# A hybrid decoder layer: the 64x64 triangular inversions as 64x64 tiles of TensorE instead of block-diagonal 128x128 operands, and another place for one group's input strips

## The chip, the cores and the metric

One Trainium2 chip, of which the kernel uses one core. The metric is the device time of one execution in microseconds (us), and lower is better. The engines are named as in the profile: PE is TensorE's matmuls and PEld its weight loads, DVE is VectorE, ACT is ScalarE, POOL is GpSimd, SP issues nearly all DMAs.

## The reference

One layer of a recurrent decoder, for a prompt of 1024 tokens and 8 sample sequences of 8 tokens. The columns of `z = x @ w_in` go to four mixers A (RG-LRU), B (Mamba-2 SSD), C (gated DeltaNet) and D (S5); their outputs are gated, joined, multiplied by `w_out`, and normalised. The change concerns C's chunked form and the order of C's and D's first steps:

```python
def gdn_mixer(...):                       # C: 4 heads of width 64, chunks of 64 tokens
    qkv, new_buf = causal_conv(qkv, ...)  # width 4, 768 channels (6 strips of 128)
    ...
    kk = jnp.einsum('bzhtd,bzhsd->bzhts', k, k)
    m = jnp.where(strict, beta[..., :, None] * kk * gamma, 0.0)
    eye = jnp.eye(c, dtype=F32)
    tmat = lax.linalg.triangular_solve(eye + m, jnp.broadcast_to(eye, m.shape),
                                       left_side=True, lower=True, unit_diagonal=True)
    value = tmat @ (beta[..., None] * v)
    kcum = tmat @ ((beta * jnp.exp(decay))[..., None] * k)
    ...                                   # then a scan over chunks with the state s

def s5_mixer(...):                        # D: 16 groups, scan, then a gate by a 256x256 product
    ...
    y = jax.nn.gelu(y.reshape(bsz, L, W_D), approximate=False)
    y = y * jax.nn.sigmoid(jnp.einsum('ble,ef->blf', y, p['s5_glu_w']) + p['s5_glu_b'])
```

## The kernel before

Tokens are laid out as 64 sample tokens and 1024 prompt tokens. `gemm_block` makes one block of `x @ w_in`: 128 output channels (a strip) by 320 or 384 tokens, 24 matmuls, three for each of eight slices of the contraction (lines 232 to 234: high by high, low by high, high by low part). A strip has three blocks, so 72 matmuls.

**The order of the work.** The program is written as Python generators. `merge` takes the next step of the generator that has used the least, by the costs that the `yield`s give, over its weight. A scheduler then orders each engine's instructions at build time, by that order and its own estimates, and each engine works its list through in order. So the order on PE is fixed, and a matmul whose operand is late holds up all matmuls behind it.

**The first third.** `u_tiles` makes D's input strips. `s5` goes on in stages that end at a `yield`: half 0's scan, half 0's outputs and half 1's scan, half 1's outputs (line 683, stored by the `ydd` transfer and read back as `yt`), and the gate (GLU, lines 707 to 730; `gh` and `gl` are the high and low parts of its operands). Beside them C's six channel strips (`strip_c`) are made in the order 2, 3, 0, 1, 4, 5, and `in_c` makes those that are still missing, and for each its convolution (`conv_of`); `norms` (line 762) takes sums of squares with matmuls of two columns.

**The long middle.** `gdn` (C) and `side` (everything else: A, B, the gates, then the projection `project`) are merged with weights 130 and 280. C works on a sample tile of 64 rows (`ti` 0) and eight prompt tiles of 128 rows (`ti` 1 to 8). Each prompt tile holds two chunks of 64 tokens: rows 0 to 63 (`lo`) and 64 to 127 (`hi`), for four heads. For a tile, `prep` makes the matrix A, `invert` inverts its 64x64 diagonal blocks, `state` and `finish` use them.

**The inversion** doubles the size of the inverted blocks in six levels (three in the sample tile). `X` and `Y` are an approximate inverse and its transpose, f16, packed as 64 columns for each head. At each level PE makes `T` from `ah` (f16 of A) and X (line 863), DVE masks it with `lev` (line 865), PE adds products to X and Y in the bank `XY` (lines 870 and 873), and ACT copies X and Y out (lines 875 and 880). The two chunks of a tile are done by one 128x128 matmul for each head, so the stationary operand has to be block-diagonal, zero outside the blocks. `ah`, `al`, `tb` and `yb` are kept for that, cleared once; `spread` (line 854, DVE, two copies) puts T into `tb`, and two ACT copies (line 878) put Y into `yb`, except at the last level. One refinement follows: `E` (lines 884, 885), `F` (line 892); then two steps that join the chunks of a tile (line 896, already 64x64, and 906, 909).

Of the kernel before, what the change touches and what calls it, by code (L numbers as in the profile page):

```python
# [10 lines left out]
F16 = mybir.dt.float16  # L11
BF = mybir.dt.bfloat16
I32 = mybir.dt.int32
AF = mybir.ActivationFunctionType
OP = mybir.AluOpType
AX = mybir.AxisListType.X
PS = bass.MemoryType.PSUM
DR = bass.MemoryType.DRAM

P = 128  # L20
NP = 1024
NS = 64
T = NP + NS
# [29 lines left out]
def hybrid_step(ctx, tc, I, O, dbg=None):  # L53
    nc = tc.nc
    mm = nc.tensor.matmul
    tr = nc.tensor.transpose
    act = nc.scalar.activation
    V = nc.vector
    G = nc.gpsimd
    tt, ts, stt = V.tensor_tensor, V.tensor_scalar, V.scalar_tensor_tensor  # L60
# [16 lines left out]
    def nm(s):  # L77
        uid[0] += 1
        return f"{s}_{uid[0]}"

    def const(shape, dt=F32, name="c"):
        n = nm(name)
        return con.tile(shape, dt, name=n, tag=n)
# [18 lines left out]
    def bank(name="p", tag="b"):  # L102
        if tag == "e":
            tag = "bisibi"[turn[0] % 6]
            turn[0] += 1
        return pm.tile([P, 512], F32, name=nm(name), tag=tag, bufs=banks[tag])

    def run(g):
        for _ in g:
            pass  # L110
# [658 lines left out]
    def gdn(wk, up, q, k, v, rk, rq):  # L769
        def r1(name, tag="r", bufs=3):  # L770
            return wk.tile([P, 256], F32, name=nm(name), tag=tag, bufs=bufs)

        def f16(name, tag, n, bufs):
            return wk.tile([P, n], F16, name=nm(name), tag=tag, bufs=bufs)
# [10 lines left out]
        ts(rq2, rq2, 1.0 / 4096, None, op0=OP.mult)  # L785
        rq8 = const([P, 9, 4], F32, "rq8")
        ts(rq8, rq, 0.125, None, op0=OP.mult)
        ah, al, tb, yb = (wk.tile([P, 4, P], F16, name=t, tag=t) for t in ("ah", "al", "tb", "yb"))
        for t in (ah, al, tb, yb):
            G.memset(t, 0.0)  # L790
        S = const([P, 2, P], F32, "S")
        V.memset(S, 0.0)

# [42 lines left out]
        def invert(d):  # L836


            n, A = d["n"], d["A"]
            nb = n // 64  # L840
            lo, hi = slice(0, 64), slice(64, P)
            blocks = (lo, hi)[:nb]
            V.tensor_copy(ah[:n, :, lo], A[:n, :, lo])
            if nb == 2:
                V.tensor_copy(ah[hi, :, hi], A[hi, :, hi])
            for s in blocks:
                tt(al[s, :, s], A[s, :, s], ah[s, :, s], OP.subtract)

            def pk(z):
                return z.rearrange("p (h t) -> p h t", h=4)  # L850

            def spread(dst, src):
                for s in blocks:
                    V.tensor_copy(dst[s, :, s], src[s])

            idq = idp[:n].unsqueeze(1)
            px = bank("XY", "i")
            pX, pY = pk(px[:, :256]), pk(px[:, 256:])
            X = Y = None
            for l in range(3 if n == NS else 6):  # L860
                pt = pk(bank("T", "i")[:, :256])
                for h in range(4):
                    mm(pt[:n, h], ah[:n, h, :n], idp[:n] if X is None else X[:n, h], start=True, stop=True)  # L863
                t_ = pk(f16("T", "T", 256, 2))
                tt(t_[:n], pt[:n], lev[:n, l].unsqueeze(1).to_broadcast([n, 4, 64]), OP.mult)  # L865
                spread(tb, t_)
                if l == 0:
                    mm(px[:n].rearrange("p (a t) -> p a t", t=64), idh[:n, :n], idq.to_broadcast([n, 8, 64]), start=True, stop=False, skip_group_check=True)
                for h in range(4):
                    last = mm(pY[:n, h], tb[:n, h, :n], idp[:n] if Y is None else Y[:n, h], start=False, stop=h == 3, skip_group_check=True)  # L870
                with tc.issue_after(last.ins):
                    for h in range(4):
                        mm(pX[:n, h], idh[:n, :n] if Y is None else yb[:n, h, :n], t_[:n, h], start=False, stop=False, skip_group_check=True)  # L873
                X = pk(f16("X", "X", 256, 2))
                act(X[:n], pX[:n], AF.Copy)  # L875
                if l < (2 if n == NS else 5):
                    for s in blocks:
                        act(yb[s, :, s], pY[s], AF.Copy)  # L878
                Y = pk(f16("Y", "Y", 256, 2))
                act(Y[:n], pY[:n], AF.Copy)  # L880
                yield 0.2
            pe = pk(bank("E", "i")[:, :256])
            for h in range(4):
                mm(pe[:n, h], ah[:n, h, :n], X[:n, h], start=True, stop=False)
                mm(pe[:n, h], al[:n, h, :n], X[:n, h], start=False, stop=True)
            for s in blocks:
                tt(tb[s, :, s], pe[s], idp[s].unsqueeze(1).to_broadcast([64, 4, 64]), OP.subtract)
            yield 0.5
            pf = bank("F", "i")
            pF, pX1 = pk(pf[:, :256]), pk(pf[:, 256:])  # L890
            for h in range(4):
                mm(pF[:n, h], tb[:n, h, :n], Y[:n, h], start=True, stop=True)
            Yf = wk.tile([P, 4, P], F32, name=nm("Yf"), tag="py", bufs=3)
            if nb == 2:
                for h in range(4):
                    mm(pX1[lo, h], Y[lo, h], tb[lo, h, lo], start=True, stop=True)
            for s in blocks:
                tt(Yf[s, :, s], Y[s], pF[s], OP.subtract)
            yield 0.3
            if nb == 2:  # L900
                x1 = pk(r1("x1", "kh", 1))
                tt(x1[lo], X[lo], pX1[lo], OP.subtract)
                pj = bank("J", "i")
                pT_, pY_ = pk(pj[:, :256]), pk(pj[:, 256:])
                for h in range(4):
                    mm(pT_[hi, h], A[lo, h, hi], x1[lo, h], start=True, stop=True)
                act(x1[hi], pT_[hi], AF.Copy, scale=-1.0)
                for h in range(4):
                    mm(pY_[lo, h], x1[hi, h], Yf[hi, h, hi], start=True, stop=True)
                act(Yf[lo, :, hi], pY_[lo], AF.Copy)  # L910
                G.memset(Yf[hi, :, lo], 0.0)
                yield 0.9
            d["Y"] = Yf
# [323 lines left out]
    u_run, s5_run = u_tiles(), s5(dp)  # L1237
# [8 lines left out]
    idh = const([P, P], F16, "idh")  # L1246
# [3 lines left out]
    idp = const([P, 64], F16, "idp")  # L1250
# [17 lines left out]
    for l in range(6):  # L1268
        m = 1 << l
        nb = 64 // (2 * m)  # L1270
# [16 lines left out]
    z, early_z = {}, (2, 3, 0, 1, 4, 5)  # L1287

    def strip_c(i):
        z[i] = yield from gemm_strip(C_QKV, "cache_gdn_conv", i, cs)  # L1290

    next(s5_run)
    columns()
    for i in early_z[:1]:
        run(strip_c(i))
    next(s5_run)
    for i in early_z[1:3]:
        run(strip_c(i))
    next(s5_run)
    run(s5_run)  # L1300
    dec_c = decays(raw[:, :, 8:12], hv[:, 4:8], nega[:, 4:8])
    dec_b = decays(raw[:, :, 0:4], hv[:, 0:4], nega[:, 0:4])
# [31 lines left out]
    wk = ctx.enter_context(tc.tile_pool(name="wk", bufs=1, reuse_waits="tile"))  # L1334
# [215 lines left out]
```

## Time and profile before

| what | before |
|---|---|
| device time, median of 3 runs (lowest to highest) | 604.24 us (603.3 to 605.51) |
| the profiled execution: device time, span of its instructions | 608.82 us, 607.1 us |
| PE busy | 582.5 us (96%), 4284 matmuls |
| PEld busy | 505.9 us (83%) |
| DVE busy | 461.9 us (76%) |
| ACT busy | 320.7 us (53%) |
| mean granted TensorE clock | 0.979 |

All figures but the first row are of one profiled execution. Busy PE includes the time in which a matmul's result is still on its way through the array, so several matmuls are counted at once: how far PE is from its pace is seen in the distances between the starts of matmuls. A matmul with f32 operands that aren't rounded to the "fp32r" form stands twice in the trace.

### The profile page before, as it was taken

How to read it: one execution, taken by the hardware profiler on the slowest of the kernel's cores; microseconds unless marked ns; L12 is line 12 of the kernel's file. 1: busy time of each engine (PE TensorE's matmuls, PEld its weight loads, DVE VectorE, ACT ScalarE, POOL GpSimd, SP SyncE). 2: the span in 40 equal slices, each digit the busy share in tenths (PEclk: the TensorE clock that was granted, in tenths of full speed). 3: DMA queues.
4: the chain of work that ended last, by engine and by line, in shares of the span. 5: the costliest groups of instructions: out<-in, count | busy, mean ns of one | idle time of the engine just before them, and what ended most of it. 6: DMA issues, size and time to landing. Idle time of an engine off the chain costs nothing.

```text
span 607.1 us, 11704 instructions
## 1 busy us (share of the span) xinstructions
PE 582.5 (96%) x4284; PEld 505.9 (83%) x4284; DVE 461.9 (76%) x1372; ACT 320.7 (53%) x877; POOL 57.1 (9%) x165
## 2 busy tenths in 40 slices
PE   5999899998999999999999999999999999999995
PEld 4999899998999886888988888788887876888883
DVE  6997969964548676688887986878796879766655
ACT  5555245345335365979575575767666566222210
POOL 8120000000100010120010010010101001000000
PEclk9999899999789999999999999999999979999998
DMA  8552122041401110001032310100104132221221
GB/s 300 181 157 80 55 64 87 19 125 60 141 18 44 33 37 36 18 19 36 2 101 68 112 32 18 36 28 3 52 1 153 36 124 90 86 105 70 108 101 70
DMA packets 24186, 44.14 MB, mean 73 GB/s; under 512 B 3200, under 2 KB 10432, under 8 KB 24128
## 3 DMA queue, kind: packets, MB, share of 16 engines
q1 hardware_dynamic: 24128, 43.38, 21.8%
q8 instruction: 34, 0.56, 0.4%
q14 instruction: 24, 0.20, 0.1%
HBM read 32.97 MB, written 10.41 MB: 71 GB/s over the span
## 4 chain that ended last, share of the span: by engine, by line
PE 72%; DVE 15%; ACT 5%; issue 3%; DMA 3%; POOL 1%; SPq 1%; DVEq 0%; ACTq 0%; POOLq 0%
PE pg L233 8%; PE pg L232 8%; PE pg L234 8%; PE pg L1443 6%; PE pg L1442 6%; PE pg L1444 6%; PE kq L825 2%; PE ssq L762 1%; DMA wr<-in_w_tiles_dram 1%; DVE acc L268 1%; PE cb L1107 1%; PE pg L405 1%; DVE cm L471 1%; PE pg L406 1%; PE pg L407 1%
## 5 line engine op out<-in xcount | busy, mean ns | idle before, releaser
L232 PE MATMUL pg<-xh,wh 128*128 128x384 f32 (+1 forms) x432 | 149.4, 346 | 0.0
L233 PE MATMUL pg<-xl,wh 128*128 128x384 f32 (+1 forms) x432 | 148.2, 343 | 0.0
L234 PE MATMUL pg<-xh,wl 128*128 128x384 f32 (+1 forms) x432 | 148.0, 343 | 0.0
L232 PEld LDWEIGHTS pg<-xh,wh 128*128 128x128 f32 x432 | 83.1, 192 | 2.7 <-issue 1.3
L234 PEld LDWEIGHTS pg<-xh,wl 128*128 128x128 f32 x432 | 82.8, 192 | 1.7 <-issue 0.8
L233 PEld LDWEIGHTS pg<-xl,wh 128*128 128x128 f32 x432 | 83.0, 192 | 1.1 <-issue 0.3
L1443 PE MATMUL pg<-wol,wh 128*128 128x512 f32 (+1 forms) x144 | 57.6, 402 | 0.0
L1442 PE MATMUL pg<-woh,wh 128*128 128x512 f32 (+1 forms) x144 | 57.6, 401 | 0.0
L1444 PE MATMUL pg<-woh,wl 128*128 128x512 f32 (+1 forms) x144 | 57.6, 401 | 0.0
L268 DVE SCALAR_TENSOR_TENSOR acc<-z,pcol,acc 128x1112 f32<-128x1112 f32 x36 | 49.3, 1372 | 3.3 <-ACT acc L266 3.0
L156 ACT ACTIVATE wh<-wr 128x512 fp32r<-128x512 f32 (+1 forms) x40 | 25.3, 634 | 39.1 <-PE pg L233 32.6
L875 ACT ACTIVATE X<-XY 128x256 f16<-128x256 f32 (+1 forms) x51 | 19.6, 385 | 27.4 <-PE XY L873 27.3
L1444 PEld LDWEIGHTS pg<-woh,wl 128*128 128x128 f32 (+1 forms) x144 | 26.6, 184 | 7.4 <-issue 0.4
L1442 PEld LDWEIGHTS pg<-woh,wh 128*128 128x128 f32 (+1 forms) x144 | 26.5, 184 | 7.4 <-ACT woh L1407 0.4
L1443 PEld LDWEIGHTS pg<-wol,wh 128*128 128x128 f32 (+1 forms) x144 | 26.5, 184 | 7.3 <-issue 0.6
L246 ACT ACTIVATE z<-pg 128x384 f32<-128x384 f32 (+2 forms) x48 | 17.4, 394 | 25.7 <-PE pg L234 24.0
L878 ACT ACTIVATE yb<-XY 64x256 f16<-64x256 f32 x82 | 30.5, 372 | 0.8
L865 DVE TENSOR_TENSOR T<-T,lev 128x256 f16<-128x256 f32 (+1 forms) x51 | 21.5, 421 | 11.4 <-PE T L863 10.2
L157 DVE TENSOR_TENSOR wl<-wr,wh 128x512 fp32r<-128x512 f32 (+1 forms) x40 | 27.8, 694 | 2.0 <-ACT wh L156 1.8
L1445 DVE SCALAR_TENSOR_TENSOR y<-y,pg 128x512 f32<-128x512 f32 (+1 forms) x18 | 12.3, 683 | 15.8 <-PE pg L1444 15.8
L405 PE MATMUL pg<-wh,xh 128*128 128x268 f32 x72 | 21.4, 298 | 2.7 <-ACT bg L410 2.7
L1458 ACT ACTIVATE y<-y,nb,rs 128x1024 f32<-128x1024 f32 (+1 forms) x8 | 10.0, 1244 | 23.9 <-DVE nb L1457 12.8
(444 smaller groups left out, 1334.1 us busy)
## 6 DMA issues: line engine op xcount, KB each, us to landing
wr<-in_w_tiles_dram SPq DMA_DIRECT2D x40, 256.0 KB, 2.8
x<-in_x_t_dram SPq DMA_DIRECT2D x8, 544.0 KB, 4.8
wo<-in_w_out_dram SPq DMA_DIRECT2D x16, 256.0 KB, 3.0
y<-in_x_dram SPq DMA_DIRECT2D x8, 512.0 KB, 3.2
out_y_dram<-y SPq DMA_DIRECT2D x7, 512.0 KB, 2.6
bgd<-bg SPq DMA_DIRECT2D x9, 128.0 KB, 1.7
dud<-us SPq DMA_DIRECT2D x2, 544.0 KB, 4.6
U<-dud SPq DMA_DIRECT2D x16, 68.0 KB, 2.6
```

Source lines behind the costliest of these rows:

```text
L156: act(hv_, wv, AF.Copy)
L157: lo_eng[0].tensor_tensor(lv, wv, hv_.bitcast(F32), OP.subtract)
L232: mm(o, whi[k], xh[:, k, a:b], start=(k == 0), stop=False)
L233: mm(o, whi[k], xl[:, k, a:b], start=False, stop=False)
L234: mm(o, wlo[k], xh[:, k, a:b], start=False, stop=(k == 7))
L268: stt(acc[:, :CL], s[:, j:j + CL], col(wkey, j * nt + i), acc[:, :CL], OP.mult, OP.add)
L405: mm(o, xh[:, k, c0:c0 + P], whi[k], start=(k == 0), stop=False)
L865: tt(t_[:n], pt[:n], lev[:n, l].unsqueeze(1).to_broadcast([n, 4, 64]), OP.mult)
L878: act(yb[s, :, s], pY[s], AF.Copy)
L1442: mm(ps[:n], mh[k_], woh[:, k_, e], start=(k_ == 0), stop=False)
L1443: mm(ps[:n], mh[k_], wol[:, k_, e], start=False, stop=False)
L1444: mm(ps[:n], ml[k_], woh[:, k_, e], start=False, stop=(k_ == 7))
```

## The change

The inversion's products no longer run on the whole array. Each head's product is made as two 64x64 products, `lo` in the array's first rows and columns and `hi` in its last, one behind the other (`each`). So every group of four matmuls is now one of eight, and `tb`, `yb`, `spread`, the two ACT copies into `yb` and the clearing of the four tiles are gone. X's products now stand ahead of Y's. A level's cost for `merge` is 0.4 where it was 0.2. Apart from that, C's strips are made beside S5's stages as 1, 2, 0 and 2: five strips ahead of `in_c` where there were three.

```diff
-        ah, al, tb, yb = (wk.tile([P, 4, P], F16, name=t, tag=t) for t in ("ah", "al", "tb", "yb"))
-        for t in (ah, al, tb, yb):
-            G.memset(t, 0.0)
...
-            V.tensor_copy(ah[:n, :, lo], A[:n, :, lo])
-            if nb == 2:
-                V.tensor_copy(ah[hi, :, hi], A[hi, :, hi])
-            for s in blocks:
-                tt(al[s, :, s], A[s, :, s], ah[s, :, s], OP.subtract)
...
-            def spread(dst, src):
-                for s in blocks:
-                    V.tensor_copy(dst[s, :, s], src[s])
-
-            idq = idp[:n].unsqueeze(1)
+            def each(o, lhs, rhs, **kw):
+                for h in range(4):
+                    for s in blocks:
+                        last = mm(o[s, h], lhs(s, h), rhs(s, h), **kw)
+                return last
+
+            def of(z):
+                return lambda s, h: z[s, h]
+
+            ah, al = (pk(f16(t, t, 256, 1)) for t in ("ah", "al"))
+            for s in blocks:
+                V.tensor_copy(ah[s], A[s, :, s])
+            for s in blocks:
+                tt(al[s], A[s, :, s], ah[s], OP.subtract)
+            idq = lambda s, h: idp[s]
...
-                for h in range(4):
-                    mm(pt[:n, h], ah[:n, h, :n], idp[:n] if X is None else X[:n, h], start=True, stop=True)
+                each(pt, of(ah), idq if X is None else of(X), start=True, stop=True)
                 t_ = pk(f16("T", "T", 256, 2))
                 tt(t_[:n], pt[:n], lev[:n, l].unsqueeze(1).to_broadcast([n, 4, 64]), OP.mult)
-                spread(tb, t_)
...
-                for h in range(4):
-                    last = mm(pY[:n, h], tb[:n, h, :n], idp[:n] if Y is None else Y[:n, h], start=False, stop=h == 3, skip_group_check=True)
+                last = each(pX, idq if Y is None else of(Y), of(t_), start=False, stop=False, skip_group_check=True)
                 with tc.issue_after(last.ins):
-                    for h in range(4):
-                        mm(pX[:n, h], idh[:n, :n] if Y is None else yb[:n, h, :n], t_[:n, h], start=False, stop=False, skip_group_check=True)
-                X = pk(f16("X", "X", 256, 2))
+                    each(pY, of(t_), idq if Y is None else of(Y), start=False, stop=False, skip_group_check=True)
+                X, Y = (pk(f16(t, t, 256, 2)) for t in "XY")
                 act(X[:n], pX[:n], AF.Copy)
-                if l < (2 if n == NS else 5):
-                    for s in blocks:
-                        act(yb[s, :, s], pY[s], AF.Copy)
-                Y = pk(f16("Y", "Y", 256, 2))
                 act(Y[:n], pY[:n], AF.Copy)
-                yield 0.2
+                yield 0.4
...
-    for i in early_z[:1]:
+    for n in (1, 2, 0):
+        for i in early_z[len(z):len(z) + n]:
+            run(strip_c(i))
+        next(s5_run, None)
+    for i in early_z[len(z):len(z) + 2]:
         run(strip_c(i))
-    next(s5_run)
-    for i in early_z[1:3]:
-        run(strip_c(i))
-    next(s5_run)
     run(s5_run)
```

Three places of the order on the engines show what moves. The first is PE's list inside the inversion of the second prompt tile, level 1: `T` is the product's bank, `pg` a block of a strip of `side`; the last figure is the output's rows by columns. Before:

```order
L234 MATMUL pg_3495<-xh,wl_3291 128x384
L863 LDWEIGHTS ah
L863 MATMUL T_3366<-X_3346,ah 128x64
L863 LDWEIGHTS ah
L863 MATMUL T_3366<-X_3346,ah 128x64
L863 LDWEIGHTS ah
L863 MATMUL T_3366<-X_3346,ah 128x64
L863 LDWEIGHTS ah
L863 MATMUL T_3366<-X_3346,ah 128x64
L232 MATMUL pg_3495<-xh,wh_3290 128x384
```

And now (the group has eight pairs of a load and a matmul, behind a strip matmul; its last three pairs are shown, with what follows):

```order
L847 LDWEIGHTS ah_3401
L847 MATMUL T_3454<-X_3437,ah_3401 64x64
L847 LDWEIGHTS ah_3401
L847 MATMUL T_3454<-X_3437,ah_3401 64x64
L847 LDWEIGHTS ah_3401
L847 MATMUL T_3454<-X_3437,ah_3401 64x64
L233 MATMUL pg_3441<-xl,wh_3330 128x384
L234 MATMUL pg_3441<-xh,wl_3331 128x384
```

Four matmuls of the whole array have become eight of a quarter of it, and strip matmuls of the whole array still stand on both sides. Counted along the whole of PE's list, neighbours that use array tiles of different sizes number 178 before and 366 after, 188 more.

The second place is DVE's list at the same levels; `acc` is a convolution step over 1112 columns. Before:

```order
L865 TENSOR_TENSOR T_3371<-T_3366,lev_873 128x256
L1006 TENSOR_TENSOR oss_3712<-oss_3712,rq_407_2318 128x4
L268 SCALAR_TENSOR_TENSOR acc_4125<-z_3012,pcol_96,acc_4125 128x1112
L854 COPY tb<-T_3371 64x4x64 x2
L951 SCALAR_TENSOR_TENSOR R_3576<-ks_3571,nea_2316,vt_3178 128x64 x4
```

And now:

```order
L866 TENSOR_TENSOR T_3417<-T_3408,lev_873 128x256
L1213 SCALAR_TENSOR_TENSOR gi_3254<-gi_3254,acc_2802 128x1112
L268 SCALAR_TENSOR_TENSOR acc_4246<-z_2931,pcol_96,acc_4246 128x1112
L866 TENSOR_TENSOR T_3463<-T_3454,lev_873 128x256
L268 SCALAR_TENSOR_TENSOR acc_4246<-z_2931,pcol_96,acc_4246 128x1112
```

Between a level's mask and its next products there was a second visit to DVE, here behind a convolution step; now there is one visit.

The third place is PE's list ahead of D's gate (`glu`). Before:

```order
L233 MATMUL pg_2138<-xl,wh_2107 128x384
L234 MATMUL pg_2138<-xh,wl_2108 128x384
L725 MATMUL glu_1721<-gh_1712,gh_1708 128x320
L725 MATMUL glu_1729<-gh_1712,gh_1708 128x384
L725 MATMUL glu_1737<-gh_1712,gh_1708 128x384
L725 MATMUL glu_1748<-gh_1712,gh_1708 128x320
```

And now:

```order
L232 MATMUL pg_1936<-xh,wh_1879 128x384
L233 MATMUL pg_1936<-xl,wh_1879 128x384
L725 MATMUL glu_1721<-gh_1712,gh_1708 128x320
L725 MATMUL glu_1729<-gh_1712,gh_1708 128x384
L725 MATMUL glu_1737<-gh_1712,gh_1708 128x384
L725 MATMUL glu_1748<-gh_1712,gh_1708 128x320
```

Between the last of half 1's outputs (line 683) and the gate stood 96 strip matmuls before, and stand 140 now. The matmuls of the sums of squares (line 762, each of which stands twice in a trace) came behind the gate in runs of 18, 9 and 9, and come now in runs of 27 and 9.

## Rows read from the trace of the kernel before

**Rows 1.** The page: busy time of each engine, and the chain by engine.

```profile
PE 582.5 (96%) x4284; PEld 505.9 (83%) x4284; DVE 461.9 (76%) x1372; ACT 320.7 (53%) x877; POOL 57.1 (9%) x165
...
PE 72%; DVE 15%; ACT 5%; issue 3%; DMA 3%; POOL 1%; SPq 1%; DVEq 0%; ACTq 0%; POOLq 0%
```

**Rows 2.** Windows, the middle: length, then busy us of PE, PEld, DVE, ACT, POOL.

```profile
200.00:490.00 290.00, 284.85 (x2537) 238.84 (x2535) 230.69 (x649) 190.00 (x572) 26.60 (x67) 1.00 0.14 44
```

**Rows 3.** Groups by form: busy us, mean ns of one, idle before and its releaser.

```profile
L870 PE MATMUL XY<-Y,tb 128*128 128x64 f16 x160 | 11.5, 195 | 2.3 <-DVE tb L854 2.3
...
L878 ACT ACTIVATE yb<-XY 64x256 f16<-64x256 f32 x82 | 30.5, 372 | 0.8
...
L854 DVE COPY tb<-T 64x256 f16<-64x256 f16 x99 | 21.6, 218 | 1.0
```

**Rows 4.** Waits of PE and PEld: us in total, times, longest.

```profile
PE XY L870 <- DVE tb L854: 2.8, 6, 0.9
...
PEld L870 <- DVE tb L854: 7.7, 22, 1.2
...
PEld L863 <- issue: 5.1, 26, 0.8
```

**Rows 5.** Timeline of PE, a prompt tile's group: start, length, line, form, count.

```profile
310.20 0.34 PE L232 MATMUL pg<-xh,wh 128*128 128x384 f32 x1
310.38 0.29 PE L870 MATMUL XY<-Y,tb 128*128 128x64 f16 x4
310.51 0.28 PE L873 MATMUL XY<-T,yb 128*128 128x64 f16 x4
310.62 0.42 PE L233 MATMUL pg<-xl,wh 128*128 128x384 f32 x1
310.88 0.34 PE L234 MATMUL pg<-xh,wl 128*128 128x384 f32 x1
```

**Rows 6.** Timeline of PE, the sample tile's group, on one 64x64 tile.

```profile
204.52 0.34 PE L233 MATMUL pg<-xl,wh 128*128 128x384 f32 x1
204.79 0.31 PE L870 MATMUL XY<-idp,tb 64*64 64x64 f16 x4
204.94 0.29 PE L873 MATMUL XY<-T,idh 64*64 64x64 f16 x4
205.16 0.44 PE L234 MATMUL pg<-xh,wl 128*128 128x384 f32 x1
205.44 0.34 PE L232 MATMUL pg<-xh,wh 128*128 128x384 f32 x1
```

**Rows 7.** Timeline of PE, from F on the whole array to 64x64.

```profile
247.94 0.29 PE L892 MATMUL F<-Y,tb 128*128 128x64 f16 x4
248.16 0.31 PE L896 MATMUL F<-tb,Y 64*64 64x64 f16 x4
```

**Rows 8.** Timeline of PE, two 64x64 tiles mixed: one line's f16 and another's f32.

```profile
207.82 0.19 PE L863 MATMUL T<-X,ah 64*64 64x64 f16 x1 [0.21 <-ACT X L875]
207.83 0.27 PE L941 MATMUL ks<-S,mk 64*64 64x64 f32 x1
207.85 0.25 PE L863 MATMUL T<-X,ah 64*64 64x64 f16 x3
```

**Rows 9.** Timeline of PE, the gate's first matmuls, with PE's idle time before them.

```profile
140.47 0.91 PE L725 MATMUL glu<-gh,gh 128*128 128x320 f32 x4 [0.80 <-ACT gh L713]
141.79 0.41 PE L726 MATMUL glu<-gl,gh 128*128 128x320 f32 x1 [0.42 <-DVE gl L714]
...
143.00 0.41 PE L726 MATMUL glu<-gl,gh 128*128 128x320 f32 x1 [0.32 <-DVE gl L714]
```

**Rows 10.** Windows behind the sums of squares; after POOL's: granted clock, DMA share, GB/s.

```profile
155.40:162.20 6.80, 6.80 (x24) 6.80 (x25) 5.30 (x18) 0.63 (x1) 2.46 (x10) 0.50 0.23 77
...
169.10:172.40 3.30, 3.30 (x14) 3.30 (x14) 1.26 (x1) 0.00 (x0) 0.00 (x0) 0.50 0.25 79
```

More of the change, by code (lines that the diff above doesn't have):

```diff
@@ L861, in invert @@
                 pt = pk(bank("T", "i")[:, :256])
-                for h in range(4):
-                    mm(pt[:n, h], ah[:n, h, :n], idp[:n] if X is None else X[:n, h], start=True, stop=True)
+                each(pt, of(ah), idq if X is None else of(X), start=True, stop=True)
                 t_ = pk(f16("T", "T", 256, 2))
                 tt(t_[:n], pt[:n], lev[:n, l].unsqueeze(1).to_broadcast([n, 4, 64]), OP.mult)
-                spread(tb, t_)
                 if l == 0:
-                    mm(px[:n].rearrange("p (a t) -> p a t", t=64), idh[:n, :n], idq.to_broadcast([n, 8, 64]), start=True, stop=False, skip_group_check=True)
@@ L869, in invert @@
-                for h in range(4):
-                    last = mm(pY[:n, h], tb[:n, h, :n], idp[:n] if Y is None else Y[:n, h], start=False, stop=h == 3, skip_group_check=True)
+                    for s in blocks:
+                        mm(px[s].rearrange("p (a t) -> p a t", t=64), idp[s], idp[s].unsqueeze(1).to_broadcast([64, 8, 64]), start=True, stop=False, skip_group_check=True)
+                last = each(pX, idq if Y is None else of(Y), of(t_), start=False, stop=False, skip_group_check=True)
@@ L879, in invert @@
-                Y = pk(f16("Y", "Y", 256, 2))
                 act(Y[:n], pY[:n], AF.Copy)
-                yield 0.2
+                yield 0.4
             pe = pk(bank("E", "i")[:, :256])
             for h in range(4):
[L884 to L887, printed above, removed]
+                for s in blocks:
+                    mm(pe[s, h], ah[s, h], X[s, h], start=True, stop=False)
@@ L888, in invert @@
+                for s in blocks:
+                    mm(pe[s, h], al[s, h], X[s, h], start=False, stop=True)
+            e_ = pk(f16("E", "T", 256, 2))
+            tt(e_[:n], pe[:n], idp[:n].unsqueeze(1).to_broadcast([n, 4, 64]), OP.subtract)
             yield 0.5
@@ L890, in invert @@
             pF, pX1 = pk(pf[:, :256]), pk(pf[:, 256:])
-            for h in range(4):
-                mm(pF[:n, h], tb[:n, h, :n], Y[:n, h], start=True, stop=True)
+            each(pF, of(e_), of(Y), start=True, stop=True)
             Yf = wk.tile([P, 4, P], F32, name=nm("Yf"), tag="py", bufs=3)
@@ L895, in invert @@
                 for h in range(4):
-                    mm(pX1[lo, h], Y[lo, h], tb[lo, h, lo], start=True, stop=True)
+                    mm(pX1[lo, h], Y[lo, h], e_[lo, h], start=True, stop=True)
             for s in blocks:
```

## The prediction, made before the changed kernel ran

> **What bounds the kernel now.** I read the page first: PE is busy for 96% of the span and holds 72% of the chain that ended last [rows 1]. Such a busy share can hide waiting, so I took the windows next. In the middle, where C and `side` run together, PE is idle for 5.2 of 290 us (290.00 less 284.85), while DVE is busy for 230.69 and ACT for 190.00 [rows 2]. The reader is to see that PE sets the pace there, and that work taken from DVE or ACT is worth only what PE waited for. The list of waits says how much that is [rows 4]: PE itself stood 2.8 us in six places for the copy into `tb`; its weight loads stood 7.7 us in 22 places for the same copy, and 5.1 us in 26 places ahead of `T`, where no releaser is seen. The idle time of a weight load is partly covered by the matmul still running, so these are bounds from above. Last I read PE's timeline matmul by matmul, by the distances between starts, since there the price of a group of small matmuls among strip matmuls can be read off directly.
>
> **What goes.** DVE loses 99 copies, 21.6 us busy, and ACT 82 copies, 30.5 us busy [rows 3]. Neither bounds the stage, so this counts only through PE's waits. By the two kinds of waits above it gives back between 2.8 us (PE's own) and 12.8 us (7.7 and 5.1, if all the idle time of the loads turned into matmul time). I take 5 us: one of the two visits to DVE between T and its products is gone, but the mask's visit stays, still queued behind convolution steps, and so does ACT's copy of X. POOL's four clearings go as well, and POOL is idle for 91% of the span [rows 1], so nothing is gained there.
>
> **What comes: the visits.** This is the main term. Groups of small matmuls stand among strip matmuls that use the whole array. Before, a prompt tile's group also used the whole array. From the start of the strip matmul ahead of a group of eight to the start of the second one behind it took 310.88 - 310.20 = 0.68 us [rows 5]. The sample tile's group is the same eight products with 64 rows, so it ran on a 64x64 tile of the array: 205.44 - 204.52 = 0.92 us [rows 6]. A visit to the 64x64 form costs 0.24 us more for the same number of matmuls, and nothing in those rows waits. Where it is lost is seen at F, whose four whole-array matmuls are followed by four of 64x64: the last of the first four started at 247.94 + 0.29 - 0.19 = 248.04, the next at 248.16, so 0.12 us where the pace inside a group is 0.03; the length of one, 0.19, is from the groups by line [rows 3, 7]. Each change of tile size costs about 0.09 us, on the way in and on the way out, and the rest is that the first matmuls on either side run slower.
>
> The number of visits comes from the order: 188 more changes of tile size, so 94 visits. The code says the same: 8 prompt tiles with six T groups, six XY groups and one E group are 104, and some stand next to a group that had the small form already. F had its visit before (line 896). So 94 x 0.24 = **22.6 us**. From below, the changes alone, 188 x 0.09 = 16.9 us.
>
> **What comes: twice the matmuls.** For each prompt tile 21 groups of four (18 in the levels, two of E, one of F) become groups of eight, so 84 x 8 = 672 matmuls more. Nothing before runs f16 pairs on two 64x64 tiles, so I bound it. If a pair overlaps, it takes as long as one: a pace of 0.03 us in either form [rows 5, 6], nothing added. If it doesn't, each added matmul takes 0.031 us, 20.8 us in all. The nearest rows: the f16 matmuls of line 863 start at 207.82 and 207.85 although an f32 matmul of line 941 started between them, at 207.83 [rows 8]; the second product cost the first stream nothing. I take 0 and keep 20.8.
>
> Those two lines write into different banks, while the new pairs write the upper and the lower half of one bank, and no row of before has that with two row halves. A rule of the Trainium skill speaks against the change here: TensorEngine Tiling (Array Packing), Restrictions and Gotchas, PSUM pressure, says that different row tiles cannot use the same PSUM bank at once. By the row the sum keeps its 0; by the rule pairs would follow each other and the sum would be 20.8 us longer. No run so far shows which.
>
> **What moves: the strips.** The gate's first matmuls found PE idle for 0.80, 0.42 and 0.32 us [rows 9], because `gh` and `gl` came late. Now 44 more strip matmuls stand ahead of them, at 0.17 us each [rows 5] 7.5 us of work that hides this wait: **-1.5 us**. The strips' weight loads are issued earlier on SP too, one more of them ahead of the transfer of half 1's outputs, which the gate needs; if that transfer comes later by some microseconds, the 7.5 us cover it, and beyond that the wait is back. The sums of squares are two-column matmuls that leave the array nearly empty, and behind the runs of 18 and 9 the clock was granted at 0.50, so 1.2 GHz, for 6.8 and 3.3 us; 24 and 14 matmuls ran there [rows 10]. At 0.17 us for the first and about 0.15 for the second they would have taken 4.1 and 2.1 us, so the half clock cost about 4 us. Now the runs are 27 and 9. This could save 4 or cost about 3 more; I take 0.
>
> The cost of 0.4 in `merge` lets `side` run ahead, so that the last tile's inversion now stands among the projection's matmuls instead of strip matmuls. They are whole-array matmuls too, so a visit costs the same there and they cover the waits as well: 0, and 2 us either way if the cover is thinner.
>
> **The sum.** The profiled execution took 608.8 us. 608.8 + 22.6 - 5 - 1.5 = 624.9. It lies 4.6 us above the median of the runs shown, so the forecast is 620 us, 2.6% slower. With the bounds of its own terms (16.9 to 22.6 for visits with 5 for what stands beside them, 2.8 to 12.8 for waits, -4 to 3 for the clock) this case reaches from 606 to 628.
>
> **The rivals.**
> - *Pairs follow each other.* By the rule above, or because PE can't feed two tiles that fast. The f32 rows of line 941 overlapping line 863 speak against, the shared bank for it. 620 + 20.8 = 641 us.
> - *Faster: the change of tile size is not paid when both halves are in use.* The rows that show the loss at entry use one tile alone [rows 6, 7]. If filling both halves avoids it, only the saved waits are left, at most 12.8 + 1.5 and likelier 6.5: 604.2 - 6.5 = 598 us. The point that decides is the price of a visit, 6.5 / 94 = 0.07 us; above that the change loses. Against it: the loss on the way out (0.12 us from the last small matmul to the strip matmul, 205.04 to 205.16) is in the same rows, and nothing in them depends on how much of the array was in use.
> - *Nothing measurable.* The visit's loss lies inside waits that PE would have had anyway, and the freed DVE and ACT time pays for the rest: 604 us. PE's 5.2 us of idle time in the middle [rows 2] are too few to hide 22.6.
>
> **How the numbers follow.** A measurement of this kernel can tell about 0.3% (1.8 us) from no change. Forecast case 0.73, pairs in sequence 0.10, faster 0.11, nothing 0.06. So faster 0.11, same 0.06, slower 0.83. The range leaves out the faster and the unchanged case and a little above the sequence case: 606 to 641; the forecast's own range is 606 to 628.
>
> **What would show it.** In the changed kernel's timeline: from a strip matmul to the first small one 0.27 us instead of 0.18, and 0.12 out again; the second of a pair starting within 0.02 us of the first and the next pair 0.03 us later (sequence: every matmul 0.03 apart); fewer and shorter waits of XY's loads for DVE; no idle time ahead of the gate; the windows of the middle longer by some 17 us while DVE's and ACT's busy sums fall by 21.6 and 30.5 us. The prediction is wrong if visits cost under 0.15 us, if PE waited far more for the inversion than its idle time shows, or if runs of small matmuls bring the clock down in the middle, where it is now granted in full [rows 2].

## The result, and the profile after

The changed kernel takes 628.57 us (median of 4 runs, 624.81 to 629.30) where the kernel before took 604.88 us beside it. The ratio is 1.0366, with a 95% interval of 1.0333 to 1.0399: 3.7% slower, 23.7 us. The forecast was slower, 620 us, and the time lies within its range of 606 to 641; the loss forecast was 16 us, so it was too small by a third.

The profiled execution is the fastest of the four, 624.81 us with a span of 623.1 us and a mean granted clock of 0.99; the other three have 0.98. The profiled execution of before had 0.979. So the two profiles differ by less (16.0 us of span) than the medians do, and the accounts below take the clock out. The page's lines of busy time and of the chain by engine, after [rows 1 before]:

```profile
PE 598.3 (96%) x4964; PEld 508.4 (82%) x4964; DVE 440.1 (71%) x1265; ACT 292.8 (47%) x795; POOL 57.7 (9%) x161
...
PE 80%; DVE 7%; issue 6%; ACT 3%; DMA 2%; POOL 1%; SPq 0%; DVEq 0%; POOLq 0%; ACTq 0%
```

DVE lost 21.8 us of work and ACT 27.9, nearly the sums of the removed copies [rows 3]. PE's share of the chain rose from 72% to 80% while DVE's halved: the work was taken from engines that were not the bound.

The windows after, of the middle [rows 2], of the rest, and of the one long stretch at half clock [rows 10]: length, busy time of PE, PEld, DVE, ACT and POOL, then the granted clock, DMA share and GB/s.

```profile
200.00:490.00 290.00, 285.85 (x2923) 233.81 (x2922) 193.39 (x497) 151.55 (x452) 24.72 (x56) 1.00 0.13 42
490.00:623.00 133.00, 122.22 (x712) 91.06 (x710) 89.89 (x242) 45.66 (x134) 8.84 (x13) 0.99 0.24 85
163.20:173.40 10.20, 10.20 (x42) 10.20 (x43) 2.77 (x10) 0.90 (x4) 0.25 (x2) 0.50 0.01 2
```

And before, the same rest, with a stretch at half clock in it that the profile of after doesn't have:

```profile
490.00:607.00 117.00, 108.87 (x481) 84.70 (x478) 78.62 (x204) 36.88 (x100) 6.46 (x10) 0.95 0.27 93
493.40:500.20 6.80, 6.80 (x24) 4.66 (x23) 5.05 (x11) 5.38 (x14) 0.00 (x0) 0.50 0.37 114
```

PE is idle for 4.15 us of the middle, 1 us less than before, and still C is later: the last 64x64 products of an inversion's F (line 892 after, 896 before) start at 530.0 us, where it was 490.0. The projection begins at 492.5 us before and 492.6 after, but from 490 us to the end the kernel now takes 133.1 us for 117.1, since C's last tile stands in it. PE's idle time in that rest is 10.8 us for 8.1, so most of its 16 us are time in which PE is busy.

A visit to the small form, after. This is PE's timeline at a prompt tile's X and Y products and at the next level's T, with columns as in [rows 5]:

```profile
309.58 0.34 PE L234 MATMUL pg<-xh,wl 128*128 128x384 f32 x1
309.85 0.31 PE L847 MATMUL XY<-T,Y 64*64 64x64 f16 x8
310.00 0.29 PE L847 MATMUL XY<-Y,T 64*64 64x64 f16 x8
310.22 0.44 PE L232 MATMUL pg<-xh,wh 128*128 128x384 f32 x1
310.50 0.34 PE L233 MATMUL pg<-xl,wh 128*128 128x384 f32 x1
310.68 0.34 PE L234 MATMUL pg<-xh,wl 128*128 128x384 f32 x1
310.95 0.31 PE L847 MATMUL T<-X,ah 64*64 64x64 f16 x8
```

From the strip matmul ahead to the second one behind it takes 310.50 - 309.58 = 0.92 us, against 0.68 before [rows 5] and exactly what the sample tile showed for half as many matmuls [rows 6]. The way in takes 0.27 us. The way out takes 0.12 us from the last small matmul, and the first strip matmul is followed after 0.28 us, not 0.17. Between the starts of two lines of eight lie 0.15 us, as between two lines of four on one tile [rows 6]: here the second tile's products cost nothing.

The gate's first matmuls after, where 0.80, 0.42 and 0.32 us of idle time stood before [rows 9]:

```profile
145.59 0.34 PE L233 MATMUL pg<-xl,wh 128*128 128x384 f32 x1
145.96 1.25 PE L725 MATMUL glu<-gh,gh 128*128 128x320 f32 x6
147.05 0.34 PE L234 MATMUL pg<-xh,wl 128*128 128x384 f32 x1
147.29 0.41 PE L726 MATMUL glu<-gl,gh 128*128 128x320 f32 x1
```

No row is marked with idle time. PE's waits after (us in total, times, longest); of these rows only the first two had as much before, when they were 6.2 and 2.7 us:

```profile
PE pg L381 <- ACT wh L357: 5.8, 1, 5.8
PE pg L405 <- ACT bg L410: 2.7, 1, 2.7
PE pg L1439 <- DVE wol L1404: 1.3, 3, 0.7
PE yT L1142 <- DVE y L1138: 1.3, 3, 0.6
PE pg L1438 <- ACT woh L1403: 1.2, 2, 1.0
PE kq L822 <- ACT z L246: 1.1, 2, 0.8
...
PE khT L811 <- DVE kh L802: 0.7, 1, 0.7
...
PE XY L847 <- DVE T L866: 0.5, 1, 0.5
```

The wait of XY for DVE fell from 2.8 us, for `tb` [rows 4], to 0.5, for `T`. Others came in its place, above all ahead of the projection (L1438, L1439) and of transposes outside the inversion (yT, khT).

**An account of PE's time.** To put sizes to this I added up the distances between the starts of neighbouring matmuls over the whole trace (from the first start to the last), with stretches at granted clock 0.50 counted at half, an estimate of what they would be at full clock. What a distance has over the usual one for its shape is put to a change of tile size and the matmuls beside it, to the edge of an inversion group with no change there (small waits), or, over 0.45 us, to a long wait of the inversion or of another matmul. In us:

```
kernel                          changes of tile size  edges  long waits of     products of    sum of all
                                number      cost             inversion others  the inversion  distances
before                             197      46.9       5.9       3.4     7.6       22.1         582.8
changed                            371      70.7      -1.0       0.6    13.0       24.1         604.3
strips alone                       200      48.3       6.2       3.0     6.5       22.1         583.4
an extra 64x64 product             283      58.4       3.5       4.9    14.7       22.4         600.7
T and E whole, cost 0.4            283      59.1      -0.0       0.7    11.9       23.1         593.3
T and E whole, cost 0.2            287      59.8      -0.5       2.5    14.3       23.5         596.0
changed, cost 0.2                  375      70.4      -2.0       1.6    10.1       24.3         600.5
sample tile and X1 whole           193      46.7       3.3       5.3    11.2       22.8         586.4
before, cost 0.4                   185      46.9       6.3       5.5    15.5       22.1         595.3
before, cost 0.1                   207      49.0       3.3       5.1    15.3       22.0         591.9
```

At equal clock the change costs 604.3 - 582.8 = 21.5 us: 23.8 for changes of tile size, 2.0 for the products, 5.4 for long waits of others, less 6.9 at the inversion's edges and 2.8 in its long waits. (What is left of each sum lies within 2 us of 497 in all these kernels.)

The columns of changes and of edges have to be read together. In the changed kernel nearly every edge of a group has a change, so a short wait that is left there counts with the changes. An estimate from the two traces, with each way in and out of a group held against the usual distance of its own kind, puts the inversion's short waits at 9.0 us before and 4.3 after. By it some 4.7 of the 6.9 us are waits saved, and the changes cost 21 to 22 us rather than 23.8.

### The profile page after: what moved, and what is told of

It reads as the page before. It is cut to its first block, busy times and chain, and to the rows that moved or that the text cites. A ratio compares the mean times of both kernels' runs of the same rounds, so it can differ in the third digit from the quotient of the medians.

```text
span 623.1 us, 12913 instructions
## 1 busy us (share of the span) xinstructions
PE 598.3 (96%) x4964; PEld 508.4 (82%) x4964; DVE 440.1 (71%) x1265; ACT 292.8 (47%) x795; POOL 57.7 (9%) x161
## 4 chain that ended last, share of the span: by engine, by line
PE 80%; DVE 7%; issue 6%; ACT 3%; DMA 2%; POOL 1%; SPq 0%; DVEq 0%; POOLq 0%; ACTq 0%
PE pg L232 11%; PE pg L234 11%; PE pg L233 11%; PE pg L1439 5%; PE pg L1440 5%; PE pg L1438 5%; PE XY L847 3%; PE T L847 2%; PE ssq L762 2%; PE rg L1210 1%; PE o L987 1%; PE pg L405 1%; PE w L954 1%; PE cb L1103 1%; PE pg L407 1%
## 5 line engine op out<-in xcount | busy, mean ns | idle before, releaser
L233 PE MATMUL pg<-xl,wh 128*128 128x384 f32 (+1 forms) x432 | 146.7, 340 | 0.0
L1439 PE MATMUL pg<-wol,wh 128*128 128x512 f32 (+1 forms) x144 | 58.3, 405 | 1.3 <-DVE wol L1404 1.3
L1438 PE MATMUL pg<-woh,wh 128*128 128x512 f32 (+1 forms) x144 | 57.5, 399 | 1.9 <-ACT woh L1403 1.2
L866 DVE TENSOR_TENSOR T<-T,lev 128x256 f16<-128x256 f32 (+1 forms) x51 | 21.4, 420 | 21.6 <-PE T L847 21.4
L1438 PEld LDWEIGHTS pg<-woh,wh 128*128 128x128 f32 (+1 forms) x144 | 26.2, 182 | 10.7 <-ACT woh L1403 3.3
L1439 PEld LDWEIGHTS pg<-wol,wh 128*128 128x128 f32 (+1 forms) x144 | 26.2, 182 | 8.8 <-DVE wol L1404 2.7
L744 ACT ACTIVATE gam<-gam,nac 128x128 f32<-128x128 f32 (+1 forms) x72 | 20.5, 373 | 3.7 <-PE gam L741 3.7
L847 PEld LDWEIGHTS <-ah 64*64 64x64 f16 x396 | 11.3, 107 | 13.4 <-issue 9.7
```

The lines of the kernel that those rows point to most:

```text
L233: mm(o, whi[k], xl[:, k, a:b], start=False, stop=False)
L847: last = mm(o[s, h], lhs(s, h), rhs(s, h), **kw)
L1438: mm(ps[:n], mh[k_], woh[:, k_, e], start=(k_ == 0), stop=False)
L1439: mm(ps[:n], mh[k_], wol[:, k_, e], start=False, stop=False)
```

## The experiments

The theory was the prediction's: a visit to the 64x64 form costs 0.2 us and more wherever it stands, and nothing else in the change is large. Its rivals were that the doubled matmuls, the strips, the clock or the new order of the work carry the loss. Ratios are to the kernel before, timed on the same chip (605.9 to 607.4 us), with 95% intervals.

**The 64x64 products alone, with their cost of 0.4.** The strips stand where they stood before.

```diff
-    for n in (1, 2, 0):
-        for i in early_z[len(z):len(z) + n]:
-            run(strip_c(i))
-        next(s5_run, None)
-    for i in early_z[len(z):len(z) + 2]:
+    for i in early_z[:1]:
+        run(strip_c(i))
+    next(s5_run)
+    for i in early_z[1:3]:
         run(strip_c(i))
+    next(s5_run)
```

> The 64x64 inversion and its cost of 0.4 as in the changed kernel, with the strips where they stood before. My theory: the visits carry the whole loss (94 visits at 0.22 to 0.24 us, 21 to 22 us), and the strips' new place gives back about 1.5 us at the gate; so this kernel takes 628 to 631 us, 1.5 us above the changed one, and PE's idle time ahead of the gate is back (about 1.5 us in three places). Rival: the strips' place itself costs several us, by the clock behind the sums of squares; then this kernel is 2 us or more below the changed one, 626 us or less.

Measured: 626.92 us, ratio 1.0343 (1.0311 to 1.0375). The changed kernel's ratio is 1.0366, and the intervals overlap. The loss is that of the products and the cost of 0.4 together. PE's idle time ahead of the gate is back (0.9 and 0.7 us), but its 1.5 us can't be made out in the time.

**The strips alone.** The opposite edit, in the kernel before.

```diff
-    for i in early_z[:1]:
...
+    for n in (1, 2, 0):
...
```

> The kernel before with only the strips moved to 1, 2, 0, 2. My theory: -1.5 us for the gate's wait and nothing else, 602 to 604 us, a ratio of 0.996 to 1.000. Rival: the runs of sums of squares, now 27 and 9, lengthen the stretch at half clock; then 606 to 609 us, ratio above 1.003.

Measured: 605.9 us, ratio 1.0000 (0.9977 to 1.0024). The three idle times ahead of the gate are gone (long waits of others 6.5 us for 7.6), but the changes of tile size and the projection's waits rose by about as much. So the strips' part is worth nothing that the times can tell, neither the gain forecast nor the loss of the rival.

**The order inside a group.** The four products of `lo` first, then the four of `hi`.

```diff
-                for h in range(4):
-                    for s in blocks:
+                for s in blocks:
+                    for h in range(4):
                         last = mm(o[s, h], lhs(s, h), rhs(s, h), **kw)
```

> The changed kernel with each group of eight in another order: the four products of lo, then the four of hi, so that neighbours use the same 64x64 tile. In the changed kernel's timeline the second of a pair started 0.004 us after the first and a pair took 0.031 us. My theory: this overlap comes from neighbours on different tiles, so now each of 1256 matmuls takes 0.031 us but where the tile changes: about 3 x 0.03 us more in each of some 160 groups of eight, 14 to 20 us more than the changed kernel, 642 to 648 us. Rival: PE overlaps the two tiles whatever the order within a few matmuls, or the pace was not what set the group's time; then within 3 us of the changed kernel.

Measured: 627.8 us, ratio 1.0354 (1.0319 to 1.0389), the same as the changed kernel. My theory of this run fell. PE's timeline of it:

```profile
310.34 0.33 PE L234 MATMUL pg<-xh,wl 128*128 128x384 f32 x1
310.60 0.32 PE L847 MATMUL XY<-T,Y 64*64 64x64 f16 x8
310.75 0.32 PE L847 MATMUL XY<-Y,T 64*64 64x64 f16 x8
310.99 0.44 PE L232 MATMUL pg<-xh,wh 128*128 128x384 f32 x1
```

Eight products still take 0.15 us, where eight in sequence at 0.031 would take 0.25. Inside the group the starts came in two interleaved series, each with a pace of 0.03 us and the second 0.013 us behind the first, where it is 0.003 in the changed kernel. The trace doesn't name the tile of a matmul; that the two series are the two tiles is read from their pace, which is that of one tile [rows 6]. So read, `hi` doesn't wait for the three `lo` products that are queued ahead of it.

**A visit added to the kernel before.** Head 3's product of `lo` once more behind each T group, as a 64x64 product.

```diff
                 for h in range(4):
-                    mm(pt[:n, h], ah[:n, h, :n], idp[:n] if X is None else X[:n, h], start=True, stop=True)
+                    last = mm(pt[:n, h], ah[:n, h, :n], idp[:n] if X is None else X[:n, h], start=True, stop=True)
+                with tc.issue_after(last.ins):
+                    mm(pt[lo, 3], ah[lo, 3, lo], idp[lo] if X is None else X[lo, 3], start=True, stop=True)
```

> The kernel before with one more matmul behind each T group: head 3's product of lo once more, as a 64x64 product into the same place with the same values. It adds 51 matmuls; 48 of them (the prompt tiles') put PE into the 64x64 form and back. My theory, a visit's price: 0.12 us in, 0.12 us out in place of 0.03, and 0.02 us on the next strip matmul, 0.22 to 0.24 us each, 10.6 to 11.5 us in all: 614 to 616 us. Rival: a change of tile size costs nothing by itself and the changed kernel's loss is that of twice the matmuls; then 51 x 0.03 = 1.5 us, 605 to 606 us.

Measured: 624.53 us, ratio 1.0299 (1.0253 to 1.0345): 18 us for 51 matmuls, more than my 11. The timeline shows the visit as expected:

```profile
313.05 0.28 PE L863 MATMUL T<-X,ah 128*128 128x64 f16 x4
313.25 0.21 PE L865 MATMUL T<-X,ah 64*64 64x64 f16 x1
313.40 0.44 PE L232 MATMUL pg<-xh,wh 128*128 128x384 f32 x1
313.68 0.34 PE L233 MATMUL pg<-xl,wh 128*128 128x384 f32 x1
```

The last of the four starts at 313.05 + 0.28 - 0.19 = 313.14, so it is 0.11 us in, 0.15 us out and 0.28 us for the strip matmul behind. The account gives 11.5 us for 86 changes (58.4 - 46.9), near my price. The rest is long waits, 19.6 us for 11.0, most of them of matmuls that have nothing to do with the added one. The addition to C's chain gave the scheduler another order, and with it came more waits; that an order alone can do this is shown by the runs of the merge's cost below.

**Half of the visits taken out of the changed kernel.** T and E on the whole array with block-diagonal `ah` and `al`; X, Y and F stay on 64x64 tiles, and the copies stay gone.

```diff
-                each(pt, of(ah), idq if X is None else of(X), start=True, stop=True)
+                for h in range(4):
+                    mm(pt[:n, h], ah[:n, h, :n], idp[:n] if X is None else X[:n, h], start=True, stop=True)
...
-                for s in blocks:
-                    mm(pe[s, h], ah[s, h], X[s, h], start=True, stop=False)
...
+                mm(pe[:n, h], ah[:n, h, :n], X[:n, h], start=True, stop=False)
...
```

> The changed kernel with T and E on the whole array again (ah and al block-diagonal as before, cleared once), while X's, Y's and F's products stay on 64x64 tiles and the copies stay gone. Changes of tile size along PE's list fall from 366 to 276, 45 visits. My theory: a visit costs 0.21 to 0.22 us wherever it stands, so this kernel is 9 to 10 us below the changed one, near 618 us, a ratio of 1.018 to 1.023 to the kernel before. Rival: most of the loss is not the visits but what the reordering of C against the rest brings (waits in the projection, which begins at the same time but shares PE with C's last tile); then it stays within 4 us of the changed kernel, ratio above 1.03.

Measured: 616.4 us, ratio 1.0181 (1.0139 to 1.0224), as my theory had it: a ratio lower by 0.0185 than the changed kernel's, for 45 visits. In the account 11.6 us of changes of tile size went with 88 of them.

**Fewer visits in the kernel before.** The sample tile's matmuls on all 128 rows, and X1 on the whole array.

```diff
-                mm(pF[:n, h], tb[:n, h, :n], Y[:n, h], start=True, stop=True)
+                mm(pF[:, h], tb[:, h], Y[:, h], start=True, stop=True)
...
-                    mm(pX1[lo, h], Y[lo, h], tb[lo, h, lo], start=True, stop=True)
+                    mm(pX1[:, h], yb[:, h], tb[:, h, lo], start=True, stop=True)
...
```

> The kernel before with 64x64 forms taken out of it: the sample tile's inversion runs on all 128 rows (the rows behind its 64 hold zeros and an identity), and X1's product of lo runs on the whole array, from yb, for which ACT makes one copy more at the last level. It takes 8 visits of the sample tile and 8 of X1 away. My theory: 16 visits at 0.21 us, 3.4 us less, and up to 1 us of that given back by the copy that X1 waits for: 601 to 603.5 us where the kernel before has 605, ratio 0.994 to 0.997. Rival: a visit costs only where it delays C's own chain, or its loss was cover for a wait; then no change, ratio 0.998 to 1.002.

Measured: 609.81 us, ratio 1.0069 (1.0048 to 1.0091), slower. The run didn't test what I meant: the account finds 193 changes of tile size for 197, not 32 fewer, since the groups now have other neighbours in small forms. What it shows instead is 5.5 us more of long waits, from an edit that adds eight short copies on ACT and no matmul.

**A visit with nobody waiting for it, and its control.** In the kernel before, one more matmul ahead of each of the 54 strip blocks, in the 64x64 form (first line added) or over the whole array (second).

```diff
+        mm(o[0:64, 0:64], whi[0][0:64, 0:64], xh[0:64, 0, a:a + 64], start=True, stop=True)
...
+        mm(o[:, 0:64], whi[0], xh[:, 0, a:a + 64], start=True, stop=True)
```

> The kernel before with one more matmul ahead of each of the 54 strip blocks, a 64x64 product into the block's bank that the block's first matmul then overwrites. It has nothing to do with the inversion and nobody waits for it. It makes 98 changes of tile size (49 visits) more than the next kernel. My theory: a visit costs 0.2 us by itself, so this kernel is 9 to 11 us above the next one. Rival: the loss in the changed kernel and in the kernel with an extra product behind T comes through C's chain; then the two differ by 1 us at most.

> The control for the kernel with a 64x64 product ahead of each strip block: the same extra matmul, but over the whole array, 128x64. Both theories: 54 matmuls at 0.03 to 0.06 us, 1.6 to 3.2 us above the kernel before, and 9 to 11 us below the one with 64x64 by mine, equal to it within 1 us by the rival.

Measured: 622.45 us, ratio 1.0267 (1.0219 to 1.0315), and 615.94 us, ratio 1.0170 (1.0131 to 1.0209). The difference is 6.5 us where I expected 9 to 11. The timeline of the first, then of the control (the extra matmul is line 231):

```profile
84.05 0.34 PE L235 MATMUL pg<-xh,wl 128*128 128x384 f32 x1
84.32 0.24 PE L231 MATMUL pg<-xh,wh 64*64 64x64 f32 x1
84.49 0.44 PE L233 MATMUL pg<-xh,wh 128*128 128x384 f32 x1
84.77 0.34 PE L234 MATMUL pg<-xl,wh 128*128 128x384 f32 x1
```

```profile
79.53 0.31 PE L235 MATMUL pg<-xh,wl 128*128 128x320 f32 x1
79.68 0.19 PE L231 MATMUL pg<-xh,wh 128*128 128x64 f32 x1
79.71 0.42 PE L233 MATMUL pg<-xh,wh 128*128 128x384 f32 x1
79.97 0.34 PE L234 MATMUL pg<-xl,wh 128*128 128x384 f32 x1
```

In the first the strip ahead is followed after 0.27 us and the small one after 0.17; in the control after 0.15 (a block of 320) and 0.03. That is 0.23 to 0.26 us a visit, 12 us, and the account of the two traces has it: 12.7 us more for the changes and the small matmuls, at 97 changes more. But it also has 4.1 us less at edges and in long waits: about a third of what the visits cost stood in time in which PE would have waited for something else. The control has a price that I had not seen: a short matmul over the whole array costs 0.03 us itself, and the strip matmul behind it is followed after 0.26 us, not 0.17.

**The cost for the merge, in both forms.** The changed kernel with 0.2, and the kernel before with 0.4 and with 0.1; nothing else is edited.

```diff
-                yield 0.4
+                yield 0.2
```

> The changed kernel with a level's cost for the merge back at 0.2, so that the last tile's inversion stands ahead of the projection, as before the change; tile-size changes along PE's list stay at 365. My theory: the changed kernel's new long waits ahead of projection matmuls (3.8 us in five places) and a slower projection (1.5 us) come from C's last tile running beside it; without them 4 to 5 us less, 623.5 to 625 us, and the visits' 18 us stay. Rival: those waits come from late copies of the output weights that are late in either order, or other waits take their place; then within 2 us of the changed kernel, 626.5 to 630.

> The kernel before with a level's cost of 0.4 and nothing else: no instruction is added or removed, tile-size changes are 175 for 178, and the last tile's inversion stands among the projection's matmuls as in the changed kernel. My theory: the order alone costs waits, 3 to 6 us, 608 to 611 us, ratio 1.005 to 1.010. Rival: the order is worth nothing on its own; then 0.997 to 1.003.

> The kernel before with a level's cost of 0.1 in place of 0.2 and nothing else. At 0.4 the same kernel took 2% more, by 10 us of long waits and a slower projection. My theory: the loss at 0.4 is that of a lagging C, whose tail falls into the projection; at 0.1 C can't end earlier than it does at 0.2, where it already stands ahead of the projection, so no gain and more waits in C's chain: 605 to 609 us, ratio 0.999 to 1.005. Rival: the waits fall with the cost all along, and 0.2 was too high; then 600 to 603 us, ratio below 0.997, a kernel that beats both.

Measured: 628.46 us, ratio 1.0327 (1.0270 to 1.0384); 619.14 us, ratio 1.0203 (1.0172 to 1.0234); 612.99 us, ratio 1.0126 (1.0105 to 1.0147). For the changed kernel the cost of 0.2 is not told from 0.4 by the times, and 628.46 us lies in the rival's range. But its four executions fall apart by granted clock: 623.75 and 625.10 us at 0.988 and 0.985, as my theory had it, and 631.82 and 631.86 us at 0.972. In the profiles at equal clock it has 3.8 us less, 2.9 of them in long waits of others. So the theory fits one pair of profiles and isn't shown by the times. For the kernel before the order alone costs 12 us at 0.4 and 7 us at 0.1, with no instruction added or removed: far more than I expected, and in both directions, so it isn't the lagging tail of C alone. PE's waits at 0.4:

```profile
PE XY L870 <- DVE tb L854: 3.5, 8, 1.0
PE pg L405 <- ACT bg L410: 2.7, 1, 2.7
PE yT L1146 <- DVE y L1142: 2.5, 5, 1.4
PE pg L1442 <- ACT woh L1407: 2.1, 3, 1.1
```

yT's wait was 0.4 us in the kernel before (`PE yT L1146 <- DVE y L1142: 0.4, 2, 0.2`), and the projection (L1442) had no long one. At 0.1 the long waits are as many, 20.4 us in all.

**T and E whole, at a cost of 0.2 and with the strips of before.**

> T and E on the whole array, the other products on 64x64 tiles, with a level's cost of 0.2 and the strips where they stood before: only the form of X's, Y's and F's products and the copies that this saves differ from the kernel before. Tile-size changes are 274 for 178, 48 visits. My theory: 48 visits at 0.21 us less about 3 us of saved waits, 7 us above the kernel before, 611 to 613 us, 4 us below the same kernel with the cost of 0.4 (616.4). Rival: the order makes no difference and it stays at 615 to 618 us.

Measured: 617.02 us, ratio 1.0171 (1.0139 to 1.0203), the same as with 0.4 and the strips moved (1.0181). The rival held: in this form the order of 0.4 is as good as that of 0.2. No version that ran beats the kernel before.

## Why the prediction was right, and where its sizes were off

*What bounds the kernel.* Right. DVE and ACT lost 21.8 and 27.9 us of work, and the kernel became slower.

*The visits, 22.6 us.* Right, and shown by taking out half of them (11.6 us for 88 changes) and by adding them where nobody waits. A visit takes 0.24 us on the timeline, and the account has 23.8 us for 174 changes more, 0.27 us a visit; without the short waits that the account counts with the changes it is 21 to 22 us, 0.24 to 0.25 a visit. (The order's count was 188. The trace of PE has 198 changes before and 376 after, 178 more, with matmuls on half of the array's columns as a size of their own, and 193 more with those taken as whole ones; the account has 174. So there were 87 to 97 visits, and the 94 stands.) The Trainium skill says in TensorEngine Tiling (Array Packing), Tiling Modes, Key Properties, that changing the tiling mode drains the array. The trace agrees as far as it goes: it has 0.12 us from one matmul to the next across a change where the pace is 0.03, and doesn't show what the array does meanwhile.

*Twice the matmuls, 0.* Nearly right: 2.0 us (24.1 for 22.1). Pairs run beside each other, and the order within a group plays no part. The Trainium skill says in TensorEngine Tiling (Array Packing), Restrictions and Gotchas, PSUM pressure, that different row tiles cannot use one PSUM bank at once. That wasn't seen to cost anything here: the two halves of each group go to one bank, and the second product of a pair starts 0.003 us after the first.

*The waits given back, 5 us.* This is the term that was mis-sized, twice. The inversion's own waits fell by an estimated 7.5 us (4.7 short, 2.8 long), more than I took and within the bounds of 2.8 to 12.8 that I kept. But long waits of other matmuls rose by 5.4 us, which I had at nothing: I put the merge's cost at 0, 2 us either way, and spoke only of what covers C's last tile. The runs show that the order as a whole is what was left out. In the kernel before the same number of 0.4 costs 12 us by itself, 0.1 costs 7, and the edits that add a matmul to the T groups or change the rows of the sample tile's came with 5 to 9 us more of long waits. The place of before is one at which few matmuls wait. How much of the changed kernel's loss is due to it having left that place can't be split exactly: with the strips aside, the 64x64 form costs 3.3% between two kernels at 0.2 (1.0327) and 1.4% between two at 0.4 (1.0343 for the products alone, over 1.0203). In the traces of these last two the sums of distances are 605.2 and 595.3 us, 9.9 us apart at equal clock where the changed kernel and the kernel before are 21.5 apart. So the visits' price is much the same in PE's time, but what the whole change loses depends on which order it is held against.

*The strips, -1.5 us.* The gate's waits are gone as forecast. The kernel with the strips alone is not faster, though: the time came back as waits ahead of the projection and more changes of tile size.

*The clock, 0.* In the profiled execution the half-clock stretch behind the sums of squares is one of 10.2 us, where there were two of 6.8 and 3.3 [rows 10], so 0 as forecast. The profile of before has 10.2 us more at half clock elsewhere (66.7 to 70.1 and 493.4 to 500.2), the profile of after none, which is most of why the two profiles lie closer together than the medians. The medians differ by 2 us more than the account, and the three executions without a profile have a lower clock than the profiled one; that fits a further stretch at half clock in them, which no row of theirs shows. The kernel with the other order inside the groups has one in its middle:

```profile
337.40:344.20 6.80, 6.80 (x22) 4.37 (x20) 3.99 (x12) 2.56 (x9) 1.18 (x2) 0.50 0.28 98
```

*The sum.* Forecast were 22.6 - 5 - 1.5 = 16.1 us. At equal clock it was 23.8 + 2.0 - 9.7 + 5.4 = 21.5 by the account, or 21.6 + 2.0 - 7.5 + 5.4 with the estimate of the short waits, and 23.7 in the medians. The form behaved as the few rows said; the order of everything around it did not. The forecast's own range was not the sum of its bounds, either: with all terms at their ends they reach from 603 us (604.2 + 16.9 - 12.8 - 1.5 - 4) to 626 (604.2 + 22.6 - 2.8 - 1.5 + 3), or 631 with the 5 us beside the visits, where the text has 606 to 628. The measured 628.57 lies half a microsecond above its 628, in the part of the range kept for pairs in sequence, which did not happen; that it lies in the range is to that extent luck.

*The rivals.* Pairs in sequence: refuted by the timeline, with eight products in 0.15 us in either order. Free changes when both halves are in use: refuted, the price is the same with one tile or two [rows 6]. Hidden in waits: a third of it, where visits were added to strips, and not enough.

## What to carry to other kernels

Before splitting small products onto tiles of the array, count how often PE would change the tile size and price a change from a row that already has one; here it was about 0.12 us each, and the copies saved were on engines that weren't the bound. Freed engines only pay through the waits of the bound one, and a change that makes the scheduler order everything anew can bring as many waits as it saves. So try a number that sets the order on the old form too, before its effect is put down to the new form.

## What the runs showed of the hardware beyond that

As the starts of the run with `lo` first read, PE begins a product on one 64x64 tile while three others, ahead of it in its list, still wait for their turn on another tile: 0.013 us after the first of them, with a pace of 0.03 us on each tile. And a short matmul among long ones costs more than its own time even in the same tile size: 0.03 us itself and 0.09 us more between the two long ones behind it (0.26 for 0.17).
